# Hybrid DeltaNet and sparse-attention trunk: the delta rule's back half for two groups at once, and three early column blocks of the output projection

## The chip, the cores and the metric

The kernel runs on one core of one Trainium2 chip. The metric is the device time of one execution in microseconds (us). The shapes are fixed: 256 tokens, model width 2048, everything in 32-bit floats.

## The reference

Two layers: a gated DeltaNet mixer, then a sparse-attention mixer, each with a residual and a squared-ReLU MLP behind it. The change lies in the DeltaNet mixer, whose core is this:

```python
for each of the 32 value heads (a key head serves two), in chunks:
    l_mat = strict_lower(beta * (k @ k.T) * decay)
    t_mat = inverse(eye + l_mat)                 # unit lower triangular
    u, w  = t_mat @ (beta * v), t_mat @ (beta * k * exp(gc))
    o     = q_dec @ state + intra @ (u - w @ state)
o   = rms_norm(o, out_norm) * silu(z)
out = concat(o over the 32 heads) @ w_out        # 4096 x 2048
```

## The kernel before

**Products in three parts.** Every weight arrives by DMA as 128x1024 floats, ACT casts it to a high part (`whi`), DVE subtracts to get the low part (`wlo`), and TensorE multiplies high by high, high by low and low by high. `Stream.get` (line 141) does this three items ahead of use, with four buffers for each part, so ACT and DVE prepare an item while TensorE works on one fetched earlier. `by_channel` (line 352) and `by_token` (line 370) consume the items and add up in PSUM tiles called `acc`, of which there are four.

**The mixer's first stage.** The loop over 16 groups of two value heads (line 714) projects a group's q, k, v (`by_channel`, 192 matmuls) and z (`by_token`, 96 matmuls), and hands the group to a generator `delta` (line 512). Its front half does the convolution, the decays `E` and the products k·k and q·k in the PSUM tiles `pk0` and `pk1`, giving `la`, the transposed v (`r`) and the scales. Its back half, from line 601, inverts the triangular matrix: a diagonal of 32x32 blocks is inverted by four levels of doubling, each with two batches of 16 matmuls of 32x32 (`Lm` and `Tc` into PSUM, ACT copies to `Pm`; `Tct` and `Pm` into PSUM, DVE subtracts into `Tc` and transposes into `Tct`). Two more 32x32 batches (8 and 12 matmuls) join the blocks to 64x64, two batches of four 64x64 matmuls join those to 128x128 (`Tt`). Then follow 128x128 products (`yv`, `o`), the norm (`so`, `f`, with the reciprocal root on POOL), the gate, a transposition of `o` and a split into the tile pair `h`, which is what the output projection reads. That is ten 32x32 batches and two 64x64 batches for each group.

**What sets the order.** Each engine runs its instructions in program order, and the program is written by a planner while the kernel is built. `Pace` (line 28) holds an assumed clock for each engine and adds an assumed cost for each instruction. `Background` (line 85) holds the generators, three active at a time. After every few streamed matmuls `tick` (line 119) advances each generator whose next step is due by that clock. `ensure` (line 338) forces steps when a tile is needed that no generator has produced yet.

**The projection's start.** The last group's output comes late. So `two_chunks` (line 389) does the first 28 of 32 row blocks of column blocks 0 and 1, which need only groups 0 to 13, and then the last four row blocks of both; `add_mix_out` (line 240) puts the weights into the stream in that order. These matmuls are 128x512. They fill the four `acc` tiles. The loop at line 804 then adds each column block to the residual (`chunk_done`, line 746: DVE adds, ACT squares), computes blocks 2 and 3 whole, and transposes the residual for the MLP in `transposed`, through `aux` PSUM tiles and, from line 738 on, `pk0` and `pk1` as well.

Of the kernel before, what the change touches and what calls it, by code (L numbers as in the profile page):

```python
# [7 lines left out]
F32 = mybir.dt.float32  # L8
# [19 lines left out]
class Pace:  # L28
# [4 lines left out]
    def __init__(self):  # L33
        self.free = {"pe": 0.0, "act": 0.0, "dve": 0.0, "pool": 0.0}
        self.chain, self.pool_end, self.last = None, 0.0, None
# [4 lines left out]
    def note(self, name, op, args, kwargs):  # L40
# [133 lines left out]
def tile_hybrid_trunk(ctx: ExitStack, tc: tile.TileContext, a: dict, out: bass.AP):  # L174
# [9 lines left out]
    htp = ctx.enter_context(tc.tile_pool(name="htp", bufs=16))  # L184
# [55 lines left out]
    def add_mix_out(w, nk):  # L240
        late = nk - 4
        for c, k0, k1 in ((0, 0, late), (1, 0, late), (0, late, nk), (1, late, nk), (2, 0, nk), (3, 0, nk)):
# [34 lines left out]
    add_mix_out(s_o, 16)  # L277
# [50 lines left out]

    def h_tile():
        return htp.tile([P, 4, T], F32, name="h")  # L330
# [138 lines left out]
    with tc.tile_pool(name="delta", bufs=2, reuse_waits="tile") as dp:  # L469
        gl_dram = dramp.tile([DN_H, T], F32, name="gl_dram")  # L470

# [40 lines left out]
        def delta(g, s, zg):  # L512
# [32 lines left out]
            while g > 1 and ("o", 2 * g - 4) not in ready:  # L545
                yield
# [23 lines left out]
            units = [(i, b) for i in range(2) for b in range(2)]  # L570
            line = lambda x: x.rearrange("p i b c -> p (i b c)")
            rows = lambda q, n=1: slice(B * q, B * (q + n))
            Lc = dp.tile([P, 4, B], F32, name="Lc")
            Lm = dp.tile([P, len(LEVELS), 4, B], F32, name="Lm")
            Tc = dp.tile([P, 4, B], F32, name="Tc")
            Tct = dp.tile([P, 4, B], F32, name="Tct")
            Pm = dp.tile([P, 4, B], F32, name="Pm")
            Tt = dp.tile([P, 2, 2, P], F32, name="Tt")
            pool.memset(Tt, 0.0)
            la = (dp.tile([P, 2, 2, T], F32, name="la0"), dp.tile([P, 2, 2, P], F32, name="la1"))  # L580
# [4 lines left out]
            for b in range(2):  # L585
                for q in range(4):
                    act.copy(Lc[rows(q), b::2], la[b][rows(q), :, 0, rows(q)])
# [6 lines left out]
            r = dp.tile([P, 2, 2, P], F32, name="r")  # L594
# [6 lines left out]
            each = lambda x: x.unsqueeze(1).to_broadcast([P, 4, B])  # L601
# [3 lines left out]
            dve.transpose(Tc.rearrange("p u c -> p (u c)"), Tct.rearrange("p u c -> p (u c)"))  # L605
            pool.tensor_tensor(Lm, Lc.unsqueeze(1).to_broadcast([P, n_l, 4, B]),
                               fine[:, 2:].unsqueeze(2).to_broadcast([P, n_l, 4, B]), op=OP.mult)
            yield True
            small_bank = lambda: aux()[:, 0:4 * B].rearrange("p (u c) -> p u c", u=4)
            for n in range(n_l):  # L610
                t = small_bank()
                for u in range(4):
# [5 lines left out]
                for u in range(4):  # L618
# [3 lines left out]
                dve.transpose(Tct.rearrange("p u c -> p (u c)"), Tc.rearrange("p u c -> p (u c)"))  # L622
                yield
            fold = Lm.rearrange("p n u c -> p (n u c)")
            T64 = fold[:, 0:256].rearrange("p (u c) -> p u c", u=4)
            P64 = fold[:, 256:512].rearrange("p (u c) -> p u c", u=4)
            Ttu = Tt.rearrange("p i b c -> p (i b) c")
            t = small_bank()
            for u, (i, b) in enumerate(units):
                for q in (0, 2):  # L630
                    pe.matmul(t[rows(q + 1), u], lhsT=la[b][rows(q), i, 0, rows(q + 1)], rhs=Tc[rows(q), u], start=True, stop=True)
# [9 lines left out]
            for u in range(4):  # L641
# [7 lines left out]
            t = aux()[:, 0:256].rearrange("p (u c) -> p u c", u=4)  # L649
            for u, (i, b) in enumerate(units):  # L650
                pe.matmul(t[rows(2, 2), u], lhsT=la[b][rows(0, 2), i, 0, rows(2, 2)], rhs=T64[rows(0, 2), u], start=True, stop=True)
            act.copy(P64[rows(2, 2)], t[rows(2, 2)])
            yield
            t = aux()[:, 0:256].rearrange("p (u c) -> p u c", u=4)
            for u in range(4):
# [4 lines left out]
            yv = dp.tile([P, 2, 2, P], F32, name="yv")  # L660

            def solve(b):
                t = aux()
                for i in range(2):
                    pe.matmul(t[:, i * P:i * P + P], lhsT=Tt[:, i, b], rhs=r[:, i, b], start=True, stop=True)
                act.copy(yv[:, :, b], t[:, :T].rearrange("p (i d) -> p i d", i=2))
# [4 lines left out]
            for i in range(2):  # L671
                pe.matmul(t[:, i * P:i * P + P], lhsT=la[0][:, i, 0, P:T], rhs=yv[:, i, 0], start=True, stop=True)
            dve.tensor_tensor(r[:, :, 1], r[:, :, 1], t[:, :T].rearrange("p (i d) -> p i d", i=2), op=OP.subtract)
# [4 lines left out]
            t = aux().rearrange("p (i b d) -> p i b d", i=2, b=2)  # L678
            for i in range(2):
                pe.matmul(t[:, i, 0], lhsT=la[0][:, i, 1, 0:P], rhs=yv[:, i, 0], start=True, stop=True)  # L680
                pe.matmul(t[:, i, 1], lhsT=la[0][:, i, 1, P:T], rhs=yv[:, i, 0], start=True, stop=False)
                pe.matmul(t[:, i, 1], lhsT=la[1][:, i, 1, :], rhs=yv[:, i, 1], start=False, stop=True)
            so = small_tile(4, "so")
            o = fold.rearrange("p (i b c) -> p i b c", i=2, b=2)
            act.copy(line(o), line(t))
            for i, b in units:
                act.activation(yv[:, i, b], o[:, i, b], AF.Square, accum_out=so[:, 2 * i + b:2 * i + b + 1])
            yield
            sc = small_tile(2, "sc")
            s2 = small_tile(2, "s2")  # L690
            f = small_tile(4, "f")
            pair = lambda x: x.rearrange("p (i b) -> p i b", i=2)
            rep = lambda x: x.unsqueeze(1).to_broadcast([P, 2, 2])
            dve.tensor_scalar(sc, rs[:, 2:4], 0.25 * float(P ** -0.5), None, op0=OP.mult)
            dve.scalar_tensor_tensor(s2, sc, 4.0 / P, sc, op0=OP.mult, op1=OP.mult)
            dve.tensor_tensor(pair(so), pair(so), rep(s2), op=OP.mult)
            dve.tensor_scalar(so, so, EPS, None, op0=OP.add)
            rsqrt(f, so, 4, pool)
            pool.tensor_tensor(pair(f), pair(f), rep(sc), op=OP.mult)
            yield True  # L700
            for i, b in units:
                dve.scalar_tensor_tensor(r[:, i, b], o[:, i, b], f[:, 2 * i + b:2 * i + b + 1], zg[:, b, i * P:i * P + P],
                                         op0=OP.mult, op1=OP.mult)
            yield
            t = aux()
# [351 lines left out]
```

## Time and profile before

| | us |
|---|---|
| median of 3 runs | 2621.61 (2621.15 to 2622.31) |
| the profiled execution | 2621.18 |
| its span on the core | 2619.4 |
| PE busy in the span | 2583.4 (99%) |
| DVE busy | 1539.8 (59%) |
| ACT busy | 1288.2 (49%) |
| POOL busy | 332.9 (13%) |

The span is what the profile covers; 1.8 us of the profiled execution lie around it. PE is TensorE's matmuls. A 32-bit matmul of two 32-bit operands leaves two records in the trace, and a transposition or a matmul of split operands one, so 16 small matmuls appear as 32 records. The end of a matmul is modelled and matmuls overlap in the pipeline, so what one costs is read from the distance between starts, and a busy PE need not be a PE at its peak. The first DeltaNet stage, with the early column blocks, takes about the first 860 us.

### The profile page before, as it was taken

Reading aid. Unit: us, or ns where it says so; the run is one execution under the profiler, and the core shown is the slowest. Engines: PE = TensorE matmul, PEld = TensorE weight load, DVE = VectorE, ACT = ScalarE, POOL = GpSimd, SP = SyncE. Lnnn points to the kernel's source line nnn. Section 1 sums busy time; section 2 is a strip of 40 time slices with the busy share of each in tenths; the row PEclk is TensorE's granted clock in tenths of the full one; section 3 lists DMA queues with packets and bytes.
Section 4 is the critical chain, followed back from the end, with each engine's and each line's share of the span. In section 5 each row is a group of like instructions: output and inputs, shape, how many; then the busy total and the mean of one; then the engine's idle time right before and its main releaser. Section 6 shows DMA issues by size and latency. Waiting matters only on the chain.

```text
span 2619.4 us, 52870 instructions
## 1 busy us (share of the span) xinstructions
PE 2583.4 (99%) x21795; PEld 2356.7 (90%) x21795; DVE 1539.8 (59%) x2308; ACT 1288.2 (49%) x1992; POOL 332.9 (13%) x674
## 2 busy tenths in 40 slices
PE   7999999999999999999999999999999999999997
PEld 7999999999987899988899988898899988999886
DVE  5777677676764555554455545576555544555544
ACT  5555555555554444443344444566544433444443
POOL 0344434343441000000000000000000000000000
PEclk9999999999999999999999999999999999999999
DMA  6655455555544566666656666644566666666664
GB/s 191 187 142 146 132 150 143 154 142 142 148 165 154 183 184 195 194 199 193 194 177 188 195 192 187 185 129 147 176 192 193 194 193 193 191 187 186 193 193 137
DMA packets 325394, 455.95 MB, mean 174 GB/s; under 512 B 18280, under 2 KB 159840, under 8 KB 324768
## 3 DMA queue, kind: packets, MB, share of 16 engines
q1 hardware_dynamic: 321888, 443.85, 56.8%
q10 hardware_dynamic: 2928, 7.37, 0.8%
q8 instruction: 171, 2.80, 0.4%
q0 software_dynamic: 336, 1.34, 0.1%
q14 instruction: 71, 0.58, 0.1%
HBM read 450.37 MB, written 2.13 MB: 173 GB/s over the span
## 4 chain that ended last, share of the span: by engine, by line
PE 66%; DVE 1%; ACT 0%; issue 0%; ACTq 0%; DVEq 0%
PE acc L78 64%; PE aux L78 1%; PE pk L78 1%; DVE wlo L78 0%; DVE p L78 0%; DVE score L78 0%; ACT whi L78 0%; ACT h L78 0%; ACT acc L78 0%; DVE m L78 0%; DVE nm L78 0%; DVE h L78 0%; ACT p L78 0%; DVE rs_t L78 0%; DVE rs_u L78 0%
## 5 line engine op out<-in xcount | busy, mean ns | idle before, releaser
L78 DVE TENSOR_TENSOR wlo<-raw,whi 128x1024 fp32r<-128x1024 f32 x838 | 1024.4, 1229 | 870.6 <-ACT whi L78 862.7
L78 ACT CAST whi<-raw 128x1024 fp32r<-128x1024 f32 x838 | 873.9, 1049 | 844.1 <-PE acc L78 813.6
L78 PE MATMUL acc<-whi,h 128*128 128x512 f32 x2816 | 887.6, 392 | 2.1 <-ACT acc L78 2.1
L78 PE MATMUL acc<-xhi,whi 128*128 128x256 f32 x3088 | 876.1, 284 | 0.3 <-ACT whi L78 0.3
L78 PE MATMUL acc<-xhi,wlo 128*128 128x256 f32 x3088 | 860.7, 279 | 0.5 <-DVE wlo L78 0.5
L78 PE MATMUL acc<-xlo,whi 128*128 128x256 f32 x3088 | 861.1, 279 | 0.0
L78 PEld LDWEIGHTS acc<-whi,h 128*128 128x128 f32 x2816 | 528.8, 188 | 111.8 <-ACT acc L78 2.9
L78 PEld LDWEIGHTS acc<-xhi,wlo 128*128 128x128 f32 x3088 | 585.2, 190 | 0.8 <-DVE wlo L78 0.8
L78 PEld LDWEIGHTS acc<-xhi,whi 128*128 128x128 f32 x3088 | 581.3, 188 | 4.6 <-ACT whi L78 0.7
L78 PEld LDWEIGHTS acc<-xlo,whi 128*128 128x128 f32 x3088 | 582.2, 189 | 0.2
L78 PE MATMUL acc<-wlo,h 128*128 128x512 f32 x1408 | 548.3, 389 | 0.0
L78 PEld LDWEIGHTS acc<-wlo,h 128*128 128x128 f32 x1408 | 264.6, 188 | 52.7
L78 PE MATMUL acc<-whi,xhi 128*128 128x256 f32 (+2 forms) x576 | 173.7, 302 | 0.0
L78 PE MATMUL acc<-whi,xlo 128*128 128x256 f32 (+2 forms) x576 | 166.5, 289 | 0.0
L78 PE MATMUL acc<-wlo,xhi 128*128 128x256 f32 (+2 forms) x576 | 166.2, 289 | 0.0
L78 POOL DMA_DIRECT2D gain<-in_norm_final x1 | 0.6, 639 | 979.1 <-ACT p L78 979.1
L78 POOL TENSOR_SCALAR E<-R,tokc 128x128 f32<-128x128 f32 x96 | 88.1, 931 | 249.0 <-DMA R<-gl_dram 226.8
L78 DVE SCALAR_TENSOR_TENSOR y<-s,cw,y 128x255 f32<-128x255 f32 (+2 forms) x192 | 93.5, 488 | 41.4 <-ACT y L78 36.8
L78 PEld LDWEIGHTS acc<-whi,xhi 128*128 128x128 f32 x576 | 108.0, 187 | 3.6
L78 PEld LDWEIGHTS acc<-wlo,xhi 128*128 128x128 f32 x576 | 108.3, 188 | 1.3
L78 PEld LDWEIGHTS acc<-whi,xlo 128*128 128x128 f32 x576 | 108.1, 188 | 1.2
L78 POOL TENSOR_TENSOR h<-h,gain 128x512 f32<-128x512 f32 x8 | 10.1, 1284 | 776.9 <-ACT acc L78 776.9
(245 smaller groups left out, 1944.3 us busy)
## 6 DMA issues: line engine op xcount, KB each, us to landing
raw<-in_mlp_w_up SPq DMA_DIRECT2D x256, 512.0 KB, 4.4
raw<-in_mlp_w_down SPq DMA_DIRECT2D x256, 512.0 KB, 4.3
raw<-in_dn_w_in SPq DMA_DIRECT2D x66, 512.0 KB, 4.2
raw<-in_dn_w_in SPq DMA_DIRECT2D x256, 128.0 KB, 2.8
raw<-in_dn_w_in SPq DMA_DIRECT2D x128, 256.0 KB, 3.2
raw<-in_dn_w_out SPq DMA_DIRECT2D x64, 512.0 KB, 3.8
raw<-in_dsa_w_out SPq DMA_DIRECT2D x32, 512.0 KB, 4.1
raw<-in_dsa_w_uq SPq DMA_DIRECT2D x16, 512.0 KB, 3.7
```

The lines of the kernel that those rows point to most:

```text
L78: r = f(*args, **kwargs)
```

## The change

`delta` now keeps only the front half. Its results `la`, `r`, the scales and the gate go into a list by pair of groups, with three buffers for `la` and `r` and five for the gate `zg`. The second group of a pair goes on into a new generator `solved`, which does the back half for both groups: every batch holds the units of four heads, so there are 32 matmuls (or 16 and 24 for the joining batches, 8 for the 64x64 ones) where there were 16 (8, 12 and 4). Its own tiles have one buffer, so a pair starts when the one before it is done; some tiles are shared (`Pm` is `Lc`, `Lm` lies in `yv`, `o` in `Tt`).

`early_chunks` takes the place of `two_chunks`: in the DeltaNet mixer three column blocks do their first 28 row blocks early, the third in `pk0` and `pk1`; these serve as extra `aux` tiles only from column block 3 on. The two last of 16 `h` tiles move to a second pool on the side that the first stage's inputs leave free. The attention mixer keeps two early blocks. The planner's cost of small matmuls is another one.

```diff
-                cost = {32: 0.039, 64: 0.084}.get(kwargs["lhsT"].shape[0], max(0.218, n / 587.0))
+            elif kwargs["lhsT"].shape[0] < P:
+                cost = {32: 0.011, 64: 0.06}[kwargs["lhsT"].shape[0]] + (0.0 if self.tiled else 0.2)
...
-    htp = ctx.enter_context(tc.tile_pool(name="htp", bufs=16))
+    htp = [ctx.enter_context(tc.tile_pool(name="htp", bufs=14))]
...
-    add_mix_out(w_o, 32)
+    add_mix_out(w_o, 32, 3)
...
-    def two_chunks(tiles, key, nk):
+    def early_chunks(tiles, key, nk, banks=()):
 
-        outs = [by_token(nk // 2 - 2, h_part(tiles), key) for _ in range(2)]
+        outs = [by_token(nk // 2 - 2, h_part(tiles), key, outs=o) for o in (None, None, *banks)]
         return [by_token(2, h_part(tiles), key, outs=o, k0=nk - 4) for o in outs]
...
-            while g > 1 and ("o", 2 * g - 4) not in ready:
+            while g > 2 and ("o", 2 * g - 5) not in ready:
...
+            p, j = g // 2, g % 2
+            la, r = (dp.tile([P, 2, 2, T], F32, name="la0", bufs=3), dp.tile([P, 2, 2, P], F32, name="la1", bufs=3)), dp.tile([P, 2, 2, P], F32, name="r", bufs=3)
+            pairs.setdefault(p, []).append((la, r, rs, zg))
...
+            if j == 1:
+                yield from solved(p, *zip(*pairs[p]))
+
+        def solved(p, la, r, rs, zg):
+
+            H, U = range(4), [(i, b) for i in range(4) for b in range(2)]
+            n_u = len(U)
+            while p and ("o", 4 * p - 1) not in ready:
+                yield
...
             for n in range(n_l):
                 t = small_bank()
-                for u in range(4):
+                for u in range(n_u):
                     for q in range(4):
                         pe.matmul(t[rows(q), u], lhsT=Lm[rows(q), n, u], rhs=Tc[rows(q), u], start=True, stop=True)
                 act.copy(Pm, t)
                 yield
...
-                dve.transpose(Tct.rearrange("p u c -> p (u c)"), Tc.rearrange("p u c -> p (u c)"))
+                dve.transpose(flat(Tct), flat(Tc))
...
+            for u, (i, b) in enumerate(U):
+                dve.scalar_tensor_tensor(o[:, i, b], o[:, i, b], f[:, u:u + 1], zg[i // 2][:, b, (i % 2) * P:(i % 2) * P + P],
                                          op0=OP.mult, op1=OP.mult)
             yield
+            hT.append(h_pair())
+            for j in range(2):
+                t = aux()
+                for n, (i, b) in enumerate(U[4 * j:4 * j + 4]):
+                    pe.transpose(t[:, n * P:n * P + P], o[:, i, b], ident)
+                at = slice(2 * j, 2 * j + 2)
+                split(t, hT[p][0][:, at].rearrange("p n t -> p (n t)"), hT[p][1][:, at].rearrange("p n t -> p (n t)"), vec("out"))
+                ready.update({("o", 4 * p + 2 * j), ("o", 4 * p + 2 * j + 1)})
+                if j == 0:
+                    yield
...
-            if g > 2:
-                ensure(("o", 2 * g - 6))
-            zg = dp.tile([P, 2, T], F32, name="zg", bufs=3)
+            if g > 4:
+                ensure(("o", 2 * g - 9))
+            zg = dp.tile([P, 2, T], F32, name="zg", bufs=5)
...
-        chunks = two_chunks(hT, "o", 32)
+        chunks = early_chunks(hT, "o", 32, [[pkp.tile([P, 512], F32, name=f"pk{b}") for b in range(2)]])
...
     for c in range(4):
-        outs = chunks[c] if c < 2 else by_token(16, h_part(hT), "o")
+        if c == 3:
+            spare[:] = [None, "pk0", None, "pk1"]
+        outs = chunks[c] if c < 3 else by_token(16, h_part(hT), "o")
```

Three places show what moves on PE, where `x16` counts matmuls of the program. In the first, PE works on the early column blocks while the last doubling level of the last group (of the last pair) is interleaved. Before:

```order
L78 MATMUL acc<-whi,h 128x512
L78 MATMUL aux<-Tc,Lm 32x32 x16
L78 MATMUL acc<-whi,h 128x512
L78 MATMUL acc<-wlo,h 128x512
L78 MATMUL acc<-whi,h 128x512 x2
L78 MATMUL acc<-wlo,h 128x512
L78 MATMUL acc<-whi,h 128x512
L78 MATMUL aux<-Pm,Tct 32x32 x16
L78 MATMUL acc<-whi,h 128x512
```

And with the change, where `yv` is the tile in which `Lm` lies and `Lc` the one that is `Pm`:

```order
L81 MATMUL acc<-whi,h 128x512
L81 MATMUL aux<-Tc,yv 32x32 x32
L81 MATMUL acc<-whi,h 128x512
L81 MATMUL acc<-wlo,h 128x512
L81 MATMUL acc<-whi,h 128x512 x2
L81 MATMUL acc<-wlo,h 128x512
L81 MATMUL acc<-whi,h 128x512
L81 MATMUL aux<-Lc,Tct 32x32 x32
L81 MATMUL acc<-whi,h 128x512
```

A batch is twice as long and there are half as many: 80 batches of 32x32 matmuls in the program instead of 160, and 16 of 64x64 ones instead of 32.

In the second, PE is at row block 24 of column block 0, the first that reads the outputs of groups 12 and 13. `aux<-wide,Tt` are the transpositions of those outputs; the next six matmuls read what is split from them. With the change:

```order
L81 MATMUL acc<-whi,h 128x512
L81 MATMUL aux<-wide,Tt 128x128 x4
L81 MATMUL acc<-whi,h 128x512
L81 MATMUL acc<-wlo,h 128x512
L81 MATMUL acc<-whi,h 128x512 x2
L81 MATMUL acc<-wlo,h 128x512
L81 MATMUL acc<-whi,h 128x512
L81 MATMUL pk_11369<-s 128x512
L81 MATMUL pk_11370<-s 128x256
L81 MATMUL aux<-ones,y 128x1 x2
L81 MATMUL aux<-wide,Tt 128x128 x4
L81 MATMUL acc<-whi,h 128x512
```

Before, group 13's transpositions stood 84 streamed matmuls ahead of the first that read them, and the last group's, the nearest to their readers, 30 ahead. Now the first four stand directly ahead of their readers, the next four 6 ahead, and all those of the last pair 78 ahead. The work that sends groups 12 and 13 to these transpositions stands 54 streamed matmuls further up, as the last group's stood before its own.

In the third, PE ends the early column blocks and goes on to the first whole one. Before (column block 2 follows):

```order
L78 MATMUL acc<-wlo,h 128x512
L78 MATMUL acc<-whi,h 128x512
L78 MATMUL pk_12921<-wide,h 128x128 x2
L78 MATMUL aux<-wide,h 128x128 x2
L78 MATMUL acc<-whi,h 128x512
```

With the change (column block 3 follows; `pk_10903` is column block 2's own PSUM tile):

```order
L81 MATMUL pk_10903<-whi,h 128x512
L81 MATMUL acc<-whi,h 128x512
L81 MATMUL acc<-wlo,h 128x512
L81 MATMUL acc<-whi,h 128x512 x2
L81 MATMUL acc<-wlo,h 128x512
L81 MATMUL acc<-whi,h 128x512
L81 MATMUL pk_12570<-wide,h 128x128 x2
L81 MATMUL aux<-wide,h 128x128 x2
L81 MATMUL pk_12580<-wide,h 128x128 x2
L81 MATMUL acc<-whi,h 128x512
```

The transpositions of the residual, six streamed matmuls into the whole block in both, now begin in the tiles in which column block 2 has just been summed.

## Rows read from the trace of the kernel before

**Rows 1.** The page: busy time, share of the span and instructions of each engine.

```profile
PE 2583.4 (99%) x21795; PEld 2356.7 (90%) x21795; DVE 1539.8 (59%) x2308; ACT 1288.2 (49%) x1992; POOL 332.9 (13%) x674
```

**Rows 2.** Who PE waited for, 60 to 845 us: total, times, longest.

```profile
PE aux L78 <- DVE r L78: 0.3, 1, 0.3
PE aux L78 <- DVE Tc L78: 0.2, 1, 0.2
```

**Rows 3.** Groups of instructions by line, PE, whole span: records, busy us, mean ns.

```profile
L78 PE MATMUL aux<-Pm,Tct 32*32 32x32 f32 x2176 | 36.0, 194 | 0.0
...
L78 PE MATMUL aux<-Tt,Lm 64*64 64x64 f32 x128 | 10.8, 224 | 0.0
```

**Rows 4.** Timeline of PE around one batch of 16: start, us, records.

```profile
252.38 0.28 PE L78 MATMUL acc<-xhi,wlo 128*128 128x256 f32 x1
252.59 0.45 PE L78 MATMUL aux<-Tc,Lm 32*32 32x32 f32 x32
252.98 0.39 PE L78 MATMUL acc<-xhi,whi 128*128 128x256 f32 x1
253.20 0.28 PE L78 MATMUL acc<-xlo,whi 128*128 128x256 f32 x1
253.32 0.28 PE L78 MATMUL acc<-xhi,wlo 128*128 128x256 f32 x1
```

**Rows 5.** Timeline of PE around a batch of four 64x64 matmuls.

```profile
409.11 0.28 PE L78 MATMUL acc<-whi,xlo 128*128 128x256 f32 x1
409.31 0.68 PE L78 MATMUL aux<-Lm,la 64*64 64x64 f32 x8
...
410.15 0.28 PE L78 MATMUL acc<-wlo,xhi 128*128 128x256 f32 x1
```

**Rows 6.** Timeline of PE around a batch of 8 matmuls of 32x32.

```profile
401.48 0.28 PE L78 MATMUL acc<-xhi,wlo 128*128 128x256 f32 x1
401.69 0.44 PE L78 MATMUL aux<-Tc,la 32*32 32x32 f32 x16
...
402.28 0.28 PE L78 MATMUL acc<-xlo,whi 128*128 128x256 f32 x1
```

**Rows 7.** The chain that ended last, 842 to 856 us: start, us, matmuls.

```profile
843.56 12.29 PE acc L78 x54
```

**Rows 8.** Timeline of all engines where the last group's output is transposed and split.

```profile
842.04 1.14 DVE L78 SCALAR_TENSOR_TENSOR r<-Lm,f,zg 128x128 f32<-128x128 f32 x4 [1.50 <-POOL f L78]
842.53 1.02 PE L78 MATMUL aux<-wide,r 128*128 128x128 f32 x4 [0.27 <-DVE r L78]
843.09 1.22 DVE L78 TENSOR_TENSOR wlo<-raw,whi 128x1024 fp32r<-128x1024 f32 x1
843.60 0.69 ACT L78 ACTIVATE h<-aux,vecs 128x512 fp32r<-128x512 f32 x1 [1.59 <-PE aux L78]
844.32 0.75 DVE L78 SCALAR_TENSOR_TENSOR h<-aux,vecs,h 128x512 fp32r<-128x512 f32 x1
844.99 1.06 ACT L78 CAST whi<-raw 128x1024 fp32r<-128x1024 f32 x1 [0.70 <-PE acc L78]
```

**Rows 9.** Timeline where the early column blocks end and the next begins.

```profile
858.10 2.48 DVE L78 TENSOR_TENSOR h<-acc,h 128x512 f32<-128x512 f32 x4
...
858.81 0.60 ACT L78 ACTIVATE acc<-h 128x512 f32<-128x512 f32 x1 [1.89 <-DVE h L78]
...
859.44 0.58 ACT L78 ACTIVATE acc<-h 128x512 f32<-128x512 f32 x1
859.59 0.50 PE L78 MATMUL acc<-whi,h 128*128 128x512 f32 x1 [1.04 <-ACT acc L78]
...
861.11 0.38 PE L78 MATMUL pk<-wide,h 128*128 128x128 f32 x2
```

**Rows 10.** Groups by form, DVE, 20 to 860 us: the doubling levels' own work.

```profile
L78 DVE STREAM_TRANSPOSE Tct<-Tc 128x128 f32<-128x128 f32 x64 | 20.0, 312 | 2.2
...
L78 DVE TENSOR_TENSOR Tc<-Tc,aux 128x128 f32<-128x128 f32 x64 | 17.9, 280 | 5.9 <-PE aux L78 5.9
```

More of the change, by code (lines that the diff above doesn't have):

```diff
@@ L598, in delta @@
             ready.add(("v", g))
[L601 removed]
+            if j == 1:
[5 more added lines that the diff above has]
+                yield
+            rows = lambda q, n=1: slice(B * q, B * (q + n))
+            flat = lambda x: x.rearrange("p u c -> p (u c)")
+            one = lambda shape, name: dp.tile([P] + shape, F32, name=name, bufs=1)
+            Lc, Tc, Tct = (one([n_u, B], n) for n in ("Lc", "Tc", "Tct"))
+            Tt, yv = one([4, 2, P], "Tt"), one([4, 2, P], "yv")
+            Pm, fold = Lc, yv.rearrange("p i b c -> p (i b c)")
+            Lm = fold.rearrange("p (n u c) -> p n u c", n=len(LEVELS), u=n_u)
+            pool.memset(Tt, 0.0)
+            for j in range(2):
+                for b in range(2):
+                    for q in range(4):
+                        act.copy(Lc[rows(q), 4 * j + b:4 * j + 4:2], la[j][b][rows(q), :, 0, rows(q)])
+            each = lambda x: x.unsqueeze(1).to_broadcast([P, n_u, B])
             n_l = len(LEVELS)
@@ L617, in delta @@
                 t = small_bank()
-                for u in range(4):
+                for u in range(n_u):
                     for q in range(4):
@@ L640, in delta @@
             t = small_bank()
-            for u in range(4):
+            for u in range(n_u):
                 pe.matmul(t[rows(1), u], lhsT=Tct[rows(1), u], rhs=Pm[rows(1), u], start=True, stop=True)
@@ L670, in delta @@
             t = aux()
-            for i in range(2):
-                pe.matmul(t[:, i * P:i * P + P], lhsT=la[0][:, i, 0, P:T], rhs=yv[:, i, 0], start=True, stop=True)
-            dve.tensor_tensor(r[:, :, 1], r[:, :, 1], t[:, :T].rearrange("p (i d) -> p i d", i=2), op=OP.subtract)
+            for i in H:
+                pe.matmul(t[:, i * P:i * P + P], lhsT=la[i // 2][0][:, i % 2, 0, P:T], rhs=yv[:, i, 0], start=True, stop=True)
+            for j in range(2):
+                dve.tensor_tensor(r[j][:, :, 1], r[j][:, :, 1], heads(t)[:, 2 * j:2 * j + 2], op=OP.subtract)
             yield
@@ L676, in delta @@
             yield
[L678 to L694, printed above, removed]
+            so = small_tile(8, "so")
@@ new lines, in solved @@
+            o = Tt
+            for j in range(2):
+                t = aux().rearrange("p (i b d) -> p i b d", i=2, b=2)
+                for i in range(2):
+                    h_ = 2 * j + i
+                    pe.matmul(t[:, i, 0], lhsT=la[j][0][:, i, 1, 0:P], rhs=yv[:, h_, 0], start=True, stop=True)
+                    pe.matmul(t[:, i, 1], lhsT=la[j][0][:, i, 1, P:T], rhs=yv[:, h_, 0], start=True, stop=False)
+                    pe.matmul(t[:, i, 1], lhsT=la[j][1][:, i, 1, :], rhs=yv[:, h_, 1], start=False, stop=True)
+                act.copy(o[:, 2 * j:2 * j + 2].rearrange("p i b c -> p (i b c)"), t.rearrange("p i b d -> p (i b d)"))
+                for u, (i, b) in list(enumerate(U))[4 * j:4 * j + 4]:
+                    act.activation(yv[:, i, b], o[:, i, b], AF.Square, accum_out=so[:, u:u + 1])
+                yield
@@ L695, in delta @@
+            sc = small_tile(4, "sc")
+            s2 = small_tile(4, "s2")
+            f = small_tile(8, "f")
+            four = lambda x: x.rearrange("p (j i b) -> p j i b", j=2, i=2)
+            rep = lambda x: x.rearrange("p (j b) -> p j b", j=2).unsqueeze(2).to_broadcast([P, 2, 2, 2])
+            for j in range(2):
+                dve.tensor_scalar(sc[:, 2 * j:2 * j + 2], rs[j][:, 2:4], 0.25 * float(P ** -0.5), None, op0=OP.mult)
             dve.scalar_tensor_tensor(s2, sc, 4.0 / P, sc, op0=OP.mult, op1=OP.mult)
-            dve.tensor_tensor(pair(so), pair(so), rep(s2), op=OP.mult)
+            dve.tensor_tensor(four(so), four(so), rep(s2), op=OP.mult)
@@ new lines, in solved @@
+            for j in range(2):
+                t = aux()
[5 more added lines that the diff above has]
+                if j == 0:
+                    yield
```

84 lines of the change are left out of this document (32 added, 52 removed).

## The prediction

> **What bounds the kernel now.** I read the page's busy times first: PE is busy 99% of the span, DVE 59%, ACT 49%, POOL 13% [rows 1]. Then I asked who PE waits for. In the whole first stage two waits on the delta rule's results stand out and they are 0.3 and 0.2 us [rows 2]. So every other engine is hidden, and a change is worth what it takes out of PE's own instruction stream. A cut on DVE, ACT or POOL is worth nothing, unless PE comes to wait.
>
> A busy PE is not PE at its peak, so the next view is the timeline, read by distances between starts. In [rows 4] one batch of 16 small matmuls (32 records) stands in a stream of 128x256 matmuls that start 0.12 us apart (253.20 to 253.32). From the last matmul ahead of the batch to the second behind it is 253.20 - 252.38 = 0.82 us. Two ordinary steps would be 0.235, so the batch costs 0.585. Inside, the last record starts 0.45 - 0.19 = 0.26 after the first (0.19 is the duration of one record, [rows 3]), which is 31 steps of 8.3 ns. So 32 records at that step are 0.265 us, and the other 0.32 us is paid once for a batch: the first small matmul starts 0.21 behind its predecessor instead of 0.12, and the first two wide ones behind it are late again.
>
> That the rest is a price of the batch and not of its matmuls is shown by a batch half as long. Eight matmuls of 32x32 [rows 6] cost 402.28 - 401.48 - 0.23 = 0.57 us, nearly as much as 16. Its records use fewer places and start 16.4 ns apart ((0.44 - 0.19) / 15), 16 of them are 0.26, and again 0.31 is fixed. For four 64x64 matmuls [rows 5]: 1.04 - 0.235 = 0.805 us in all. Inside, (0.68 - 0.22) / 7 = 65 ns for each of 8 records is 0.52, and 0.285 is fixed.
>
> **The change part by part.** I sum against the profiled execution, 2621.2 us, 0.4 below the median of the runs (2621.6).
>
> *Longer batches.* The number of small matmuls stays. Before, ten batches of 32x32 for each of 16 groups make 160 (the 64 that read `Pm` in the levels hold 2048 of the 2176 records of that form), and two of 64x64 make 32 (128 records of one form are 16 batches of 8) [rows 3]. The order of the change has 80 and 16. All of them stand on PE, which is the path, so each batch saved is its fixed part: 80 x 0.315 + 16 x 0.285 = 25.2 + 4.6 = **29.8 us less**. I assume that records in a batch of 64 still start 8.3 ns apart. No batch of before is longer than 32 records, so this is the unshown part, and it is one of the rivals.
>
> *The same work on fewer, wider instructions of DVE, ACT and POOL.* I cost it at nothing, because it hides behind PE as it does now. Steps become longer: a doubling level's subtraction and transposition on DVE take 0.28 + 0.31 us for 128 elements [rows 10] and at most twice that for 256. If the cover is gone, PE waits for the difference, and that is priced as a rival.
>
> *Outputs of groups 12 and 13.* In the order their first transpositions stand directly ahead of row block 24, which reads them. The work that leads there stands 54 matmuls further up, as the last group's does now. Those 54 take about 12.3 us [rows 7], and now they fall short by 0.27 us of idle time [rows 8]. The change has to fall short by more, since nothing stands between transposition and reader. Let T be the start of the last matmul ahead of them. The `wlo` queued on DVE ahead of the gate's products ends at about T: its item's buffer came free 12 matmuls (2.7 us) before, then a matmul's end 0.4, a cast of 1.06 and 1.22 on DVE [rows 8]. The four products that the transpositions need follow, and from the first product to the split's high part on ACT is 843.60 - 842.04 = 1.56 us, plus 0.69. DVE meanwhile does eight products, 2 x 1.14, one `wlo`, 1.22, and the low part, 0.75: T + 4.25. The low part is first read by the third matmul, which would else start at T + 1.14 (one step 0.23, four transpositions 0.45, two steps 0.46). So PE loses 3.1 us. The next four transpositions are six matmuls and a group of `pk` products ahead of their readers, but the scales of group 15 (eleven small DVE instructions, about 2.2 us) stand ahead of their low part: 0.7 us more. **3.8 us more**, with bounds 0 (if planner and chip happen to fit) and about 6 (if the root on POOL, which the same 12.3 us cover, is late as well).
>
> *Three early column blocks.* They move 192 matmuls and add none. Before, the last group's chain ran behind the early blocks and PE waited for it once, 0.27 us of idle and some 0.4 us between starts [rows 8]. With the third block the last transpositions stand 78 matmuls, about 18 us, ahead of their readers, and that wait goes: **0.4 us less**. At the end of the early blocks PE waits for the ACT squares that free `acc`: the 1.04 us idle at 859.59 [rows 9]. This stays, since column block 3 takes the same two tiles. New is that the transpositions behind it go into `pk0` and `pk1`, which hold column block 2. They need the fifth and the sixth square. Squares start at 858.81 and 859.44, 0.63 apart, so the fifth ends at 858.81 + 4 x 0.63 + 0.58 = 861.9, where PE arrives at 861.11. That is 0.8, and 0.1 to 0.2 for the sixth: **0.9 us more**, with bounds 0 and 2. The DVE adds, 0.62 each [rows 9], are ahead of the squares. ACT's next casts come two squares later, but PE works three items ahead of its weights.
>
> *Small waits elsewhere.* The last pair's steps are only six to twelve 128x512 matmuls apart, with twice the work in each: 0.5 us.
>
> Sum: 2621.2 - 29.8 + 3.8 - 0.4 + 0.9 + 0.5 = **2596.2 us**, 1.0% faster.
>
> **The rivals.**
>
> *1. The waits come back.* Each pair has 8 doubling steps, half ended by ACT and half by DVE. If all the added DVE work (at most 0.59 us a step, 32 steps) met no cover, that would be 19 us, and the result about 2615. For it speaks that a pair may not start until the one before is out, and that the planner prices DVE below its rows. Against it: the steps mostly stand 12 or more matmuls apart (1.4 us at least), and PE waited 0.2 us in all for `Tc` [rows 2], so now there is room. I take half as typical, 2606 to 2616.
>
> *2. The batch doesn't carry the price.* If the fixed part grew with the matmuls behind one wait, nothing is won, and the new waits leave 2621.2 + 4.8 = 2626. The rows against it are those of 8 and 16 matmuls, with the same 0.31 and 0.32 [rows 4, 6].
>
> *3. Slower: a long batch runs dry.* PE may be reading its instructions ahead during the slow wide matmuls, and 16 small ones may be all that it can hold. Then the second half of each batch goes at the pace at which instructions are delivered. The bounds from rows are 16.6 ns for a matmul (two records at 8.3, no effect) and 115 ns, the step of the wide stream, which delivery keeps up with [rows 4]. The middle, 66, costs 16 x 0.049 = 0.79 us in each of 80 batches: 63 us, and a time of 2659. The change turns slower from (29.8 + 0.4 - 5.2) / 80 = 0.31 us a batch, at 36 ns a matmul. For it: no batch of before is long enough to deny it. Against it: the eight-matmul batch and the 16 one show steady steps to their last record, and the wide matmuls behind start 0.12 us after the last small one, so a batch of 16 ends with more already in hand.
>
> [...]
>
> **How the numbers follow.** The forecast, joins a little better or worse than worked out, has 0.75: 2589 (no new wait, all fixed parts saved at 0.32) to 2606. Rival 1 has 0.13, rival 2 has 0.06, rival 3 has 0.06. Two runs of this kernel can be told apart from about 0.2%, 5.2 us, so faster means below 2616.4: 0.75 + 0.13 = 0.88. Rival 2 at +0.18% is no change: 0.06. Rival 3 is slower: 0.06. The range takes the forecast's ends and the lower edge of rival 1: 2589 to 2608, which leaves out 2 in 10.
>
> **What would show it.** In the timeline after, a batch of 64 records should cost about 0.85 us, with 0.53 from its first to its last start and then 0.12 to the next wide matmul. A jump of the step inside the batch is rival 3. A first start later than 0.21 us behind the wide matmul, with DVE or ACT named as what ended the wait, is rival 1. PE's idle time should show about 3 us for `h` at row block 24 and about 1 us for a square of `acc` or `pk` at the end of the early blocks, and the wait for `r` at 842 should be gone. The forecast is wrong if PE's waits in the first stage pass 12 us or the batches cost 1.1 us.

## The result, and the profile after

The changed kernel takes **2608.7 us** (median of 4 runs, 2606.85 to 2608.99), the kernel before 2621.8 beside it: ratio **0.995** (0.9938 to 0.9963). Two later series gave 0.9952 (0.994 to 0.9965) and 0.9952 (0.9939 to 0.9964). It is faster, by 13.1 us, where the forecast's sum said 25.0. The time lies above the forecast's range, 2589 to 2608.

The page first. PE's busy time answers to [rows 1]: it fell by 24.1 us, the span only by 12.3 (2619.4 to 2607.1).

```profile
PE 2559.3 (98%) x21795; PEld 2345.4 (90%) x21795; DVE 1534.1 (59%) x2164; ACT 1272.6 (49%) x1888; POOL 304.0 (12%) x514
```

So the stream got shorter nearly as forecast, and half of it came back as idle time. Who is waited for is in the waits of PE in the first stage (us in total, times, longest), against [rows 2]:

```profile
PE aux L81 <- DVE Tc L81: 6.5, 10, 1.6
PE aux L81 <- ACT Lc L81: 1.8, 1, 1.8
PE aux L81 <- DVE E L81: 1.5, 1, 1.5
PE acc L81 <- DVE h L81: 1.2, 2, 1.0
PE acc L81 <- ACT acc L81: 1.0, 1, 1.0
PE acc L81 <- ACT h L81: 0.8, 1, 0.8
PE pk L81 <- ACT pk L81: 0.8, 1, 0.8
...
```

`h`, `pk` and the square of `acc` are the waits that were forecast. `Tc` and `Lc`, the operands of the doubling levels, are not: 0.2 us before, 8.3 now. `E`, the decays of `delta`'s front half, is no new wait: the same view of the kernel before has it too, 1.5 us once, a row that [rows 2] leaves out.

**The long batch is as forecast.** One that waits for nothing, in the timeline:

```profile
427.66 0.28 PE L81 MATMUL acc<-xhi,wlo 128*128 128x256 f32 x1
427.87 0.75 PE L81 MATMUL aux<-Lc,Tct 32*32 32x32 f32 x64
428.55 0.38 PE L81 MATMUL acc<-xhi,whi 128*128 128x256 f32 x1
428.77 0.29 PE L81 MATMUL acc<-xlo,whi 128*128 128x256 f32 x1
```

It starts 0.21 us behind its predecessor, takes 0.75 - 0.19 = 0.56 from first to last start (0.53 forecast: a record's step is 8.9 ns, not 8.3), and costs 428.77 - 427.66 - 0.235 = 0.875 us. Two batches of 32 records cost 1.17 [rows 4], so 0.295 is saved (0.315 forecast).

**The head of a pair is not.** Where a pair's levels begin (ACT's 16 copies into `Lc`, then the masks):

```profile
417.88 4.06 ACT L81 COPY Lc<-la 32x64 f32<-32x64 f32 x16
...
421.97 0.43 DVE L81 TENSOR_TENSOR Tct<-Lc,fine 128x256 f32<-128x256 f32 x1 [1.67 <-ACT Lc L81]
422.02 2.66 POOL L81 TENSOR_TENSOR yv<-Lc,fine 128x1024 f32<-128x1024 f32 x1 [5.25 <-ACT Lc L81]
422.43 2.53 DVE L81 TENSOR_TENSOR Tct<-Tct,fine 128x256 f32<-128x256 f32 x1
...
425.00 0.45 DVE L81 STREAM_TRANSPOSE Tc<-Tct 128x256 f32<-128x256 f32 x1
...
425.59 0.74 PE L81 MATMUL aux<-Tc,yv 32*32 32x32 f32 x64 [0.47 <-DVE Tc L81]
...
432.19 0.75 PE L81 MATMUL aux<-Tc,yv 32*32 32x32 f32 x64 [0.64 <-DVE Tc L81]
```

DVE's second instruction on `Tct`, an add, takes 2.53 us, its neighbour of the same size 0.43. The add ends 0.28 us behind POOL's mask product (422.02 + 2.66 = 424.68; 422.43 + 2.53 = 424.96). The product itself is not what PE waits for: it is done at 424.68, and PE comes to the batch at 425.12 (425.59 - 0.47) and waits for `Tc`. The same place before the change, and below it the group of all such adds there:

```profile
414.71 1.31 POOL L78 TENSOR_TENSOR Lm<-Lc,fine 128x512 f32<-128x512 f32 x1 [1.53 <-ACT Lc L78]
...
420.83 0.29 DVE L78 TENSOR_TENSOR Tct<-Lc,fine 128x128 f32<-128x128 f32 x1
421.16 0.29 DVE L78 TENSOR_TENSOR Tct<-Tct,fine 128x128 f32<-128x128 f32 x1
...
L78 DVE TENSOR_TENSOR Tct<-Tct,fine 128x128 f32<-128x128 f32 x16 | 4.7, 292 | 0.6
```

POOL was done 4.8 us ahead of DVE there, and no add of the 16 groups was held. Now both wait for the last of the 16 copies and start together. DVE's first product, which began 0.05 us ahead of POOL's, runs at its usual pace; the add behind it stands until POOL is done. The groups of DVE in the first stage (busy, mean ns | idle before) say that this is so in every pair, and that the other instructions on 256 elements, those of [rows 10], grew by less than half each:

```profile
L81 DVE TENSOR_TENSOR Tct<-Tct,fine 128x256 f32<-128x256 f32 x8 | 20.2, 2525 | 0.3
L81 DVE STREAM_TRANSPOSE Tct<-Tc 128x256 f32<-128x256 f32 x32 | 14.3, 445 | 1.1
L81 DVE TENSOR_TENSOR Tc<-Tc,aux 128x256 f32<-128x256 f32 x32 | 13.3, 416 | 11.6 <-PE aux L81 11.5
```

**The join at row block 24** answers to [rows 7, 8]. The forecast's chain, instruction by instruction:

```profile
762.87 0.39 PE L81 MATMUL acc<-whi,h 128*128 128x512 f32 x1
...
762.99 2.19 DVE L81 SCALAR_TENSOR_TENSOR Tt<-Tt,f,zg 128x128 f32<-128x128 f32 x8
...
763.49 1.02 PE L81 MATMUL aux<-wide,Tt 128*128 128x128 f32 x4 [0.22 <-DVE Tt L81]
764.54 0.69 ACT L81 ACTIVATE h<-aux,vecs 128x512 fp32r<-128x512 f32 x1 [0.20 <-PE aux L81]
765.10 1.22 DVE L81 TENSOR_TENSOR wlo<-raw,whi 128x1024 fp32r<-128x1024 f32 x1
...
765.28 0.50 PE L81 MATMUL acc<-whi,h 128*128 128x512 f32 x1 [0.78 <-ACT h L81]
...
766.23 0.74 DVE L81 SCALAR_TENSOR_TENSOR h<-aux,vecs,h 128x512 fp32r<-128x512 f32 x1
...
767.03 1.22 PE L81 MATMUL acc<-whi,h 128*128 128x512 f32 x2 [1.01 <-DVE h L81]
```

With T = 762.87 the low part ends at 766.97 = T + 4.10 (T + 4.25 forecast). Behind it the wide matmuls start 0.43 us apart for a while, where 0.23 is usual, and one `pk` product 0.85 us behind its predecessor, where 0.43 is usual. The view of windows (us, PE busy, granted clock, DMA share, GB/s) shows the granted clock at 0.52 in the 3 us after the one in which PE stood half the time:

```profile
763.40:767.00 3.60, 1.75 (x6) 0.93 0.45 149
767.00:770.00 3.00, 2.97 (x6) 0.52 0.55 180
```

**At the end of the early blocks** [rows 9] the two waits are there as worked out, the second for the fifth square:

```profile
888.62 0.50 PE L81 MATMUL acc<-whi,h 128*128 128x512 f32 x1 [1.01 <-ACT acc L81]
...
890.32 0.58 ACT L81 ACTIVATE pk<-h 128x512 f32<-128x512 f32 x1
...
891.08 0.44 PE L81 MATMUL pk<-wide,h 128*128 128x128 f32 x2 [0.76 <-ACT pk L81]
```

**The ledger.** I took every distance between two neighbouring starts on PE, less the median of that kind of neighbours over several profiles; what is over by more than 0.12 us I call a wait. Waits in the first stage are 4.75 us before and 19.2 after.

| step | forecast | measured |
|---|---|---|
| batches (the stream without waits, 2575.1 to 2547.5) | -29.8 | -27.6 |
| outputs ahead of row block 24 (4.7, less 0.5 that such transpositions waited before) | +3.8 | +4.2 |
| wait at 842 | -0.4 | -0.7 |
| end of the early blocks (2.1 against 1.2) | +0.9 | +0.9 |
| small waits elsewhere: level batches +8.6, `wlo` +0.9, a transposition +0.6 | +0.5 | **+10.1** |
| sum | -25.0 | -13.1 |

PE's first start to its last shrank by 12.3 us. Of the 0.8 us left over 0.2 is a longer wait behind the very first matmul; the rest is not attributed.

### The profile page after: what moved, and what is told of

It reads as the page before. It is cut to its first block, busy times and chain, and to the rows that moved or that the text cites. A ratio compares the mean times of both kernels' runs of the same rounds, so it can differ in the third digit from the quotient of the medians.

```text
span 2607.1 us, 52386 instructions
## 1 busy us (share of the span) xinstructions
PE 2559.3 (98%) x21795; PEld 2345.4 (90%) x21795; DVE 1534.1 (59%) x2164; ACT 1272.6 (49%) x1888; POOL 304.0 (12%) x514
## 4 chain that ended last, share of the span: by engine, by line
PE 90%; DVE 5%; ACT 2%; issue 1%; DMA 1%; POOL 0%; SPq 0%; ACTq 0%; DVEq 0%; POOLq 0%
PE acc L81 81%; PE aux L81 6%; PE pk L81 3%; DVE wlo L81 2%; ACT Lc L81 1%; DVE Tct L81 1%; DMA raw<-in_dn_w_in 1%; DVE y L81 1%; ACT whi L81 1%; DMA xin<-in_x 0%; DVE Tc L81 0%; ACT acc L81 0%; DVE p L81 0%; DVE h L81 0%; DVE Tt L81 0%
## 5 line engine op out<-in xcount | busy, mean ns | idle before, releaser
L81 PE MATMUL acc<-whi,h 128*128 128x512 f32 x2688 | 847.2, 392 | 4.0 <-ACT acc L81 2.0
L81 PEld LDWEIGHTS acc<-whi,h 128*128 128x128 f32 x2688 | 504.8, 188 | 111.5 <-ACT acc L81 2.9
L81 PE MATMUL acc<-wlo,h 128*128 128x512 f32 x1344 | 524.6, 390 | 0.0
L81 PEld LDWEIGHTS acc<-wlo,h 128*128 128x128 f32 x1344 | 252.7, 188 | 50.1
L81 POOL TENSOR_SCALAR E<-R,tokc 128x128 f32<-128x128 f32 x96 | 104.5, 1103 | 144.9 <-DMA raw<-in_dn_w_in 81.2
L81 POOL TENSOR_TENSOR h<-h,gain 128x512 f32<-128x512 f32 x8 | 10.1, 1282 | 777.4 <-ACT acc L81 777.4
```

Source lines behind the costliest of these rows:

```text
L81: r = f(*args, **kwargs)
```

## The experiments

My theory (A): the collision of DVE's add with POOL's product makes the levels late. Rivals: (B) the loss is the join at row block 24; (C) longer steps no longer fit the cover anyway; (D) long batches run dry. Ratios are against the kernel before in the same series.

**1. Masks on DVE (`e2_lm_dve`).** POOL's one product becomes four on DVE, so no product on POOL can collide.

```diff
-            pool.tensor_tensor(Lm, Lc.unsqueeze(1).to_broadcast([P, n_l, n_u, B]),
-                               fine[:, 2:].unsqueeze(2).to_broadcast([P, n_l, n_u, B]), op=OP.mult)
+            for n in range(n_l):
+                dve.tensor_tensor(Lm[:, n], Lc, each(fine[:, 2 + n]), op=OP.mult)
```

> The change with the level masks (the product that POOL does in 2.65 us, at the same moment at which DVE's add takes 2.53 us) done on DVE instead, level by level. Theory 'collision' (DVE's add is held by POOL's product, and DVE's delay is what PE waits for): the add falls from 2.53 to about 0.43 us, PE's waits for Tc and Lc in the first stage fall from 8.3 us to under 3, and the time from 2608.7 to 2600-2603. Theory 'planner' (doubled steps are simply longer than planned, whoever holds them): DVE gets 1.6 us more ahead of the first batch of each pair, the waits stay at 8 us or grow, and the time is 2608-2612.

2603.1 us, ratio 0.9936 (0.9923 to 0.995). The add takes 0.44 us, the waits for `Tc` and `Lc` fall from 8.3 to 3.5 (under 3 expected). But the planner laid the chain elsewhere, and the wait at row block 24 went too: this run can't tell A from B.

**2. The product in four pieces on POOL (`e1_pool_levels`).** As above, with `pool` for `dve`.

> The change with POOL's mask product cut into four, one for each level, same work on the same engine. Theory 'collision': DVE's add can go between two of POOL's four products, so it takes 1 us or less instead of 2.53, PE's waits for Tc and Lc fall from 8.3 to about 3-4 us, and the time is 2601-2605. Theory 'planner': DVE's add may change, but the waits and the time stay, 2607-2610.

2614.3 us, 0.9975 (0.9967 to 0.9984): slower than the change, and outside both ranges. The add fell to 0.85 us as expected, but the planner, which prices four POOL instructions higher, now has PE wait 6.3 us for `Tt` at row block 24.

**3. The planner told of the collision (`e3_priced`).**

```diff
             dve.tensor_tensor(Tct, Tct, each(fine[:, 0]), op=OP.add)
+            pace.free["dve"] += 2.1
+            pace.chain += 2.1
```

> The change with the planner told that DVE's add takes 2.1 us more, and nothing else; the collision stays. Theory 'collision': DVE's add still takes 2.5 us, but the first batch of a pair stands later and PE's waits for Tc and Lc fall from 8.3 to under 4 us; the time is 2602-2606, worse than without the collision because DVE still loses its 2.1 us. Theory 'planner': the second and later waits of each pair stay (0.74 us in five pairs), so the waits stay above 5 us, and the time is 2605-2609.

2611.9 us, 0.9967 (0.9955 to 0.998), again outside both ranges. The waits for `Tc` and `Lc` nearly went (0.4 us). Instead PE waits 5.4 us for `wlo`, where it was 0.7, and in the timeline it stands at row block 24:

```profile
765.75 1.17 PE L81 MATMUL aux<-wide,Tt 128*128 128x128 f32 x4 [7.39 <-DVE Tt L81]
```

**4. A joint order of the early blocks (`e4_joint`).** Row blocks 24 to 27 come behind 0 to 23 of all three column blocks, so the first reader of groups 12 and 13 stands 288 matmuls later.

```diff
-        outs = [by_token(nk // 2 - 2, h_part(tiles), key, outs=o) for o in (None, None, *banks)]
+        mid = 2 if banks else 0
+        outs = [by_token(nk // 2 - 2 - mid, h_part(tiles), key, outs=o) for o in (None, None, *banks)]
+        for o in outs if mid else ():
+            by_token(2, h_part(tiles), key, outs=o, k0=nk - 8)
```

> The change with row blocks 24 to 27 of the three early column blocks taken behind row blocks 0 to 23 of all three, so that the outputs of groups 12 and 13 are first read 288 matmuls later. If PE's waits at row block 24 are the cost that they seem (4.6 us between 762 and 774 us beyond the usual steps), those waits go and the time is 2603.5-2605. If PE merely meets them elsewhere, because group 15's front half waits for the same outputs, the time stays at 2607-2609.

2603.4 us, 0.9939 (0.9927 to 0.9952). The waits at row block 24 are gone, the add stays at 2.5 us and the waits for `Tc` at 6.8. So B is a loss by itself, of about its 4.2 us (5.3 us between the medians, 3 by the ratios, 5.6 where `e17` below does the same to `e16`).

**5. Two early blocks only (`e5_two_early`)** and **6. the third block without pairs (`e6_three_alone`, the kernel before with that alone).** The core of 5, without the two edits that follow from it; 6 is its reverse on the kernel before:

```diff
-    add_mix_out(w_o, 32, 3)
+    add_mix_out(w_o, 32, 2)
```

> The change without its third early column block. If that block is what covers the last pair's chain: five of its steps, from the last triangular products to the transpositions, come with no streamed matmul between them, and PE waits some 15 to 25 us for them; time 2622-2632, no gain left over the kernel before. If the third block is worth only the 0.4 us that the prediction gave it: 2607-2610.

> The kernel before with a third early column block and nothing else, in pk0 and pk1. By the prediction's terms: 0.4 us for the last group's wait goes, 0.9 us at the end of the early blocks comes: 2622 +- 1.5, the same as before. If the third block is itself a gain: under 2618.

2621.7 us, 1.0001 (0.9992 to 1.0011), and 2622.5, 1.0007 (0.9998 to 1.0015), the first 0.3 us under its expected range, the second inside. By itself the third block gives nothing. With pairs it holds the whole gain: without it PE waits 33 us in the stage, 14 more than with it, and half of the 14 at one place of the timeline, where the last pair's output is forced:

```profile
839.25 1.18 PE L81 MATMUL aux<-wide,Tt 128*128 128x128 f32 x4 [7.53 <-DVE Tt L81]
```

**7. Long batches in the old kernel (`e7_twice`).** Each level batch of the kernel before issues its 16 matmuls twice, so that 128 batches have 64 records; nothing else changes.

```diff
-                for u in range(4):
+                for u in (0, 1, 2, 3, 0, 1, 2, 3):
```

> The kernel before with every batch of the doubling levels issued with each of its 16 matmuls twice in the same batch (the second writes the same result), so 128 batches have 64 records. If the price is 0.32 us a batch and the rest goes with the records: 128 x (0.562 - 0.263) = 38 us more, about 2660. If the price goes with the matmuls, 0.58 us for each 16: 74 us more, about 2696. If a batch of 64 runs dry at 66 ns a matmul: 2722.

2674.0 us, 1.0202 (1.0184 to 1.0221): 53 us more. 38 of it is the records' own time: 128 x 0.299 us (0.562 from first to last start, as in the changed kernel's batches, instead of 0.263). The rest, 15 us, is mostly waits, 5.1 of them inside batches, with nothing to wait for that the profile shows. In the view of waits of the first stage:

```profile
PE aux L78 <- issue: 5.1, 7, 1.8
```

So D is real in this kernel, but in 7 of 128 batches and not in each.

**8. Combinations, all with the planner free to move.** `e8_dve_joint` is 1 and 4; `e10_dve_joint_stt` is `e8` with the planner's DVE prices brought nearer the rows; `e12_dve_joint_aux` is `e8` with `pk0` and `pk1` used for transpositions only behind column block 3; `e13_priced_joint` is 3 and 4.

```diff
+            if op == "scalar_tensor_tensor":
+                cost = 0.23 + n / 1050.0
+            elif op == "transpose":
+                cost = 0.18 + n / 960.0
...
+        outs = chunks[c] if c < 3 else by_token(16, h_part(hT), "o")
         if c == 3:
             spare[:] = [None, "pk0", None, "pk1"]
-        outs = chunks[c] if c < 3 else by_token(16, h_part(hT), "o")
```

> The mask products on DVE level by level (as in e2) and the joint order of the early blocks (as in e4). If the collision (theory A, some 8 us) and the join at row block 24 (theory B, 4.6 us) were two separate losses, the gains would add up: 2608.5 - 5.5 - 4 = 2599. But the run with the masks on DVE alone had already lost its wait at row block 24, so I expect no sum: 2600.5 to 2604, PE waits of 10 to 13 us in the stage, the add at 0.44 us. Rival: the gains are independent, 2597 to 2600.

> The change with three edits: masks on DVE (no POOL product to hold DVE's add), row blocks 24 to 27 of the early column blocks taken behind 0 to 23 of all three, and a planner that prices DVE's scalar-tensor-tensor products and 32x32 transpositions by their rows (0.23 + n/1050 us, 0.18 + n/960 us). Theory 'both': what PE still waits 0.5 us for in five pairs with the masks on DVE is DVE work that the planner thinks shorter than it is, so these waits go as well; PE's waits in the first stage fall from 19 us to 5-8 and the time is 2596-2600, 0.8-0.95% under the kernel before. Theory 'rest is elsewhere' (weights, or instructions that reach PE late): the waits stay at 11-13 us, time 2601-2604.

> As e8, and pk0 and pk1 serve as transposition tiles only behind column block 3, so that nothing there waits for the fifth and the sixth square. Theory (the prediction's term of 0.9 us): the wait for a square of pk goes and the end of the early blocks costs 1.3 us between starts as before the change; 0.5 to 1.2 us less than e8, 2599.5 to 2603. Rival: with two transposition tiles fewer PE waits for the splits behind column block 2 instead, and the time is that of e8 or up to 1 us more.

> The collision stays (the add at 2.5 us) but the planner is told of it, as in e3, and the early blocks are in the joint order. If what e3 gave back was the join at row block 24 (7.4 us) and the collision costs only because the order does not know of it, the batches' waits are under 2 us and the time is 2601 to 2605. Rival: a longer planned chain costs elsewhere whatever the order (waits for wlo, the last pair's transpositions, which now come directly ahead of their readers at the end of the early blocks): 2606 to 2612.

`e8`: 2603.7 us, 0.9933 (0.992 to 0.9945), no better than 1 or 4 alone. `e10`: 2627.7, 1.003 (1.0018 to 1.0041), a miss. The planned chains became longer than a pair's period, and `ensure` twice forced the rest of one with nothing beside it, as its view of waits shows:

```profile
PE aux L85 <- DVE Tt L85: 15.2, 2, 7.7
```

`e12`: 2609.1, 0.9955 (0.9942 to 0.9969), also a miss, 5.4 us slower than `e8`. The wait for the square of `pk` (0.8 us) went, but with two transposition tiles fewer PE waits 5.4 us for `xlo` at the end of the early blocks, so the change's 0.9 us there is the cheaper choice.

`e13`: 2610.1, 0.9957 (0.9944 to 0.9969): the batches' waits are 1.9 us, but now `wlo` is waited for 5.0 and the last outputs cost some 3. Its rival held: a longer planned chain costs elsewhere.

**9. The order held still.** In 1 to 3 and 8 the order moved with every edit. So I issued the pieces past the planner and told it the price of the one product: `e15_pool_same_order` (pieces on POOL), `e16_dve_same_order` (on DVE). TensorE's program is then, matmul by matmul, that of the changed kernel. `e17_dve_same_joint` is `e16` with the order of `e4`.

```diff
-            pool.tensor_tensor(Lm, Lc.unsqueeze(1).to_broadcast([P, n_l, n_u, B]),
-                               fine[:, 2:].unsqueeze(2).to_broadcast([P, n_l, n_u, B]), op=OP.mult)
+            for n in range(n_l):
+                dve._engine.tensor_tensor(Lm[:, n], Lc, each(fine[:, 2 + n]), op=OP.mult)
+            pace.note("pool", "tensor_tensor", (Lm,), {})
```

> POOL's mask product in four pieces, as in e1, but the planner is told the price of the one product, so TensorE's, DVE's and ACT's programs are those of the changed kernel row by row. Theory A (the collision of the add with POOL's product is what makes the levels late): the add falls from 2.53 us to about 0.85 as in e1, the waits at the level batches from 9.4 us to 5 or 6, the join at row block 24 stays at 4.5, so 3.5 to 4.5 us less than the changed kernel beside it: 2604 to 2605.5. Rival (the levels are late whatever the add does, since sixteen copies on ACT and DVE's convolution stand ahead of them): the waits move to the next batch and the time stays within 1 us of the changed kernel.

> The mask products on DVE, as in e2, again with the changed kernel's order on TensorE. Theory A: the add at 0.44 us, the level batches' waits 4 to 6 us; DVE works 1.8 us more per pair right behind the first transposition, which may cost 0.5 us for wlo. The join at row block 24 stays at 4.5 us (in e2 it went because the planner laid the chain elsewhere). So 3.5 to 5 us less than the changed kernel: 2603.5 to 2605.5. Rival as in e15: within 1 us of the changed kernel.

> e16 with the joint order of the early blocks (TensorE's order is that of e4). If the collision and the join at row block 24 are separate, their prices add: e4's gain of some 3 to 5 us and e16's of 3.5 to 5 give 2599 to 2602, and waits of 10 to 13 us in the stage. Rival: one is already contained in the other, as e2 and e8 (2603.1 and 2603.7) suggested: 2603 to 2604.5.

| | us | ratio | waits in the stage |
|---|---|---|---|
| the changed kernel, same series (`e18_after_third`) | 2608.3 | 0.9952 (0.9939 to 0.9964) | 19.8 |
| `e15` | 2605.2 | 0.9937 (0.9924 to 0.9951) | 16.7 |
| `e16` | 2603.8 | 0.9934 (0.9921 to 0.9946) | 14.4 |
| `e17` | **2598.2** | **0.9911** (0.9897 to 0.9924) | 9.7 |

The intervals of the first two rows overlap; that the waits fell by the same 3.1 us is what tells them apart. The groups of `e15` in the first stage, the add and the pieces:

```profile
L81 DVE TENSOR_TENSOR Tct<-Tct,fine 128x256 f32<-128x256 f32 x8 | 6.8, 850 | 0.3
...
L624 POOL TENSOR_TENSOR yv<-Lc,fine 128x256 f32<-128x256 f32 x32 | 31.2, 1004 | 40.7 <-ACT Lc L81 40.7
```

and the add of `e16`:

```profile
L81 DVE TENSOR_TENSOR Tct<-Tct,fine 128x256 f32<-128x256 f32 x8 | 3.5, 438 | 0.3
```

The same add on the same operands takes 2.52, 0.85 or 0.44 us, as POOL holds it up with one long product, with a short piece, or not at all. That is A shown, and its price is 4.5 us. `e15`, where POOL keeps the work, rules out that the gain is merely a freer POOL. It got 3.1 us back, 0.4 less than A expected; its level batches wait about as long as those of `e16`, and its profile has 1.5 us of waits for nothing (`issue`, below) that the one of `e16` hasn't. `e16` gained what A expected. With the join gone as well the gains add up, 4.5 + 5.6 (0.9 more than expected), and the waits of PE in the first stage of `e17` are these:

```profile
PE aux L81 <- DVE Tc L81: 3.6, 7, 1.8
PE aux L81 <- DVE E L81: 1.5, 1, 1.5
PE aux L81 <- ACT Lc L81: 1.0, 1, 1.0
PE acc L81 <- ACT acc L81: 1.0, 1, 1.0
PE pk L81 <- ACT pk L81: 0.8, 1, 0.8
PE aux L81 <- DVE h L81: 0.5, 1, 0.5
```

`e17` beats both kernels: 22.9 us under the one before, 10.1 under the changed one. That `e8`, the same work with a planner that knows the DVE price, is 5.5 us slower than `e17`, and `e1` 9 us slower than `e15`, lies in the order that the planner makes, the one thing in which the programs of each pair differ. How it costs so much is shown for `e1` (the 6.3 us for `Tt`) and not for `e8`, in whose profile 2.9 us are waits for nothing. The changed kernel once more in the series of `e8` (`e14_after_again`) took 2608.7, 0.9952 (0.994 to 0.9965).

## Why the prediction was wrong, and which of its terms held

The forecast named its own sign of being wrong, waits of PE in the first stage beyond 12 us; they are 19.2, and the time lies 0.7 us above the range.

- **What failed is the step "the same work on fewer, wider instructions of DVE, ACT and POOL. I cost it at nothing", and with it "small waits elsewhere", 0.5 us where 10.1 were measured.** The reason I gave was that the work hides behind PE as before; the level batches alone wait 8.6 us more. I compared durations and cover, and not *when* two engines start. 16 copies on ACT became one gate for DVE and POOL, which before had run 4.8 us apart. With the collision gone and the order the same (`e16`), the level batches still wait 5.0 us of 9.3, so about half is the collision.
- **The cause of the other half stays open.** It looks like rival 1, but not in its terms, which were the steps' own added DVE time. At the three places of `e17` that I followed, a level's short instruction stands behind other work of its engine. The longest, in the timeline:

```profile
241.26 1.60 DVE L81 SCALAR_TENSOR_TENSOR y<-s,cw,y 128x255 f32<-128x255 f32 x3
...
242.85 1.22 DVE L81 TENSOR_TENSOR wlo<-raw,whi 128x1024 fp32r<-128x1024 f32 x1
244.00 0.41 DVE L81 TENSOR_TENSOR Tc<-Tc,aux 128x256 f32<-128x256 f32 x1
...
244.46 0.75 PE L81 MATMUL aux<-Tc,yv 32*32 32x32 f32 x64 [1.76 <-DVE Tc L81]
```

The subtraction takes 0.41 us; ahead of it DVE is busy with the convolution (`y`) and `wlo`. No run changes that order alone, so this is a reading and not shown.

- **Longer batches: right.** The price is fixed for a batch and not for its matmuls (0.875 us for one of 64 records, 1.17 for two of 32), which settles rival 2. 27.6 us were saved of 29.8; the difference is mainly the record's step, 8.9 ns instead of 8.3.
- **Outputs of groups 12 and 13: the waits were right, the sum partly by luck.** 4.2 us were measured for 3.8, and the chain came by its own steps to 0.15 us. Of the 4.7 us there 2.9 are the waits (3.1 forecast), 1.4 is the low clock behind them, which I had not counted (0.4 of it at the `pk` product), and 0.4 lies at the reader of the second transpositions, for which 0.7 was forecast.
- **Third column block: the terms were right, the meaning was not.** Its wait at 842 went and its end cost 0.9. I priced it as a small matter of its own; `e5` and `e6` show that it is worth nothing alone and 13 us under pairs, since the last pair's chain has nowhere else to hide.
- **Rival 1's interval, 2606 to 2616, held the time,** in good part by luck: half of the added waits at the level batches come from the collision, which it did not have. **Rival 3** is there, but sporadically: of three profiles of the changed kernel one shows such a wait in the stage's batches, of 0.2 us, and 64 records take 0.56 us from first to last start, 8.9 ns a record. That is 17.8 ns for a matmul (two records), near the lower of that rival's two bounds, 16.6, and far from its middle, 66. No run shows whether PE reads its instructions ahead.

The runs show how long DVE's add takes: 2.52 us beside POOL's one product, 0.85 beside its short pieces, 0.44 without any. DVE's first product, at 0.43 us, was not held. In `e15` the pieces on POOL are longer as well, 1.00 us each where a quarter of 2.65 is 0.66. Through what the one engine holds up the other, no run shows.

## What to carry to other kernels

When a change makes instructions wider, ask for each pair of DVE and POOL instructions what releases them; if it is the same event, they can collide as here, where the add stood 2.1 us for POOL's product. Then look at what else stands ahead of each short instruction on its engine. Cover is what the last unit of work needs: two groups at once halve the number of batches, and double what must hide at the end, so the third column block and the pairing are one change and not two. Where a planner sets the order, hold the order still in an experiment, or the run measures the planner: the same edit differed by 9 us between `e1` and `e15`.

## What was not expected of the hardware

**A long run of small matmuls sometimes stalls on nothing that the profile names.** In `e7` it was 7 of 128 batches of 64 records, 5.1 us together. In `e1` the view of waits has three at a matmul into `aux`, 2.0 us, the longest inside such a batch, 1.42 us behind its 20th record; in `e15` two, 1.5 us. `e16`, `e17` and the kernel before have none in the stage. In `e2`, `e4`, `e8` and `e12` the longest is at a wide matmul, 2.1, 1.5, 2.5 and 2.2 us. The one of `e2` in its timeline stands directly behind such a batch, with the wide matmuls after it 0.21 us apart and not 0.12, much as those behind row block 24 in the changed kernel went at 0.43 and not 0.23, at a granted clock of 0.52:

```profile
337.19 0.75 PE L81 MATMUL aux<-Lc,Tct 32*32 32x32 f32 x64
340.09 0.58 PE L81 MATMUL acc<-xhi,whi 128*128 128x256 f32 x1 [2.14 <-issue]
340.47 0.41 PE L81 MATMUL acc<-xlo,whi 128*128 128x256 f32 x1
340.68 0.41 PE L81 MATMUL acc<-xhi,wlo 128*128 128x256 f32 x1
```

What causes these stalls no run shows. Whether they are also behind the wider spread of the changed kernel (2605.3 to 2611.2 in one series, where the kernel before keeps to 2620.1 to 2621.9) stays open too.
